# A two-layer hybrid trunk: the narrow projection columns beside the retention's first head, a re-ordered opening, and four output buffers

## The chip, the cores and the metric

One Trainium2 chip, one core. The metric is the device time of one execution in microseconds; lower is better. TensorE multiplies matrices into PSUM, VectorE (DVE) and ScalarE (ACT) work on tiles in SBUF and PSUM, GpSimd (POOL) does little here, and SyncE (SP) issues every DMA from one queue.

## What is computed

Two layers over 512 latent tokens and 256 context tokens, 1024 features wide. A layer modulates its input, multiplies it by one wide `w_in`, feeds the columns to three mixers (a state-space mixer, SSD; latent attention, MLA; retention), multiplies the joined results by `w_out`, and normalises.

```python
sh_l, sc_l, g_l = jnp.split(mod_l[:, None, :], 3, axis=-1)   # mod = silu(c) @ w_ada + b_ada
h_l = x * (1 + sc_l) + sh_l
parts_l = jnp.split(h_l @ w_in[i], in_splits(), axis=-1)
...
IN_WIDTHS = (SSD_WIDTH, SSD_CONV_DIM, SSD_HEADS,
             MLA_Q_LORA, MLA_KV_LORA, MLA_ROPE_DIM, MLA_WIDTH,
             RET_QK_WIDTH, RET_QK_WIDTH, RET_WIDTH, RET_WIDTH)
...
dtc = jax.nn.softplus((dt_c + dt_bias)).reshape(...)          # SSD_HEADS = 16 columns
v = v.reshape(b, n, RET_HEADS, 1, RET_V_DIM)                  # RET_WIDTH = 512 columns, 4 heads of 128
out_l = jnp.concatenate([ssd_l, mla_l, ret_l], -1) @ w_out[i]
x_new = layer_norm(ALPHA * x + g_l * out_l, ln_g, ln_b)
```

Two of the projected pieces are narrow: 16 columns `dt` of the SSD and 32 columns `kr`, the rotary part of the MLA keys. Each token's context part is computed in layer 0 and, as keys and states only, in layer 1.

## The kernel before

**Data.** Tokens are columns: features `h` lie as eight tiles `hh[k]`, `hl[k]` of 128 features x 768 tokens (256 context columns first, then 512 latent ones). Each is a split of a float32 tile into a rounded part (`hh`, type fp32r) and a remainder (`hl`), and so are weights (`wh`, `wl`). `mm3` (L145) makes a product of three matmuls: hi x hi, hi x lo, lo x hi.

**Weights.** `wslot` (L153) loads 128 x 1024 floats of weights into one of two staging buffers `wr`, rounds them on ScalarE (`wh`) and subtracts on VectorE (`wl`), with three buffers each; from the seventh call on with high priority. `pslot` (L163) does the same in buffers of a given pool. The tile framework orders each engine's instructions ahead of time; each engine then runs its own list in order, waiting on semaphores. SP's list holds all loads and stores, so a load that waits for a buffer holds those behind it.

**A projection.** `proj` (L171) keeps 128 x 128 of weights stationary and moves 512 latent and then 256 context columns of `hh`, `hl` past them, for k = 0 to 7: 24 matmuls over 512 and 24 over 256 columns. It takes accumulators from `acc`, three PSUM banks.

**The opening** (`start`, layer 0). For k = 0 to 7 `ada(0, (j, j + 8))` multiplies two 512 KB tiles of `w_ada` (`ar`) with the conditioning vector and turns the result into columns `mod`; `make_h0(k)` loads `x`, modulates it with the columns k and 8 + k, and splits it into `hh[k]`, `hl[k]`; then three projections advance by one k, with accumulators `p0` (latent) and `c0` (context). Their tiles are `M_T` (the 48 narrow columns `dt` and `kr`), `B_T` and `B_T + 2` (the SSD's B and C of the first group). `ada` for k = 0 and k = 1 come before `make_h0(0)`, and all three weights go through `wslot`.

**The dt stage** (`dt_stage`, L439). In layer 0 it takes the opening's results (`first`); in layer 1 it projects `rq0`, `rq1` and C over the latent columns (`proj_lat`, interleaved by k while the normalisation before is still writing `hh`), then the narrow tile and B with `proj_many`. ScalarE copies the narrow rows into `ms` (48 x 768), six transposes (L470) turn them to tokens by rows, and a chain on VectorE makes `dt`, cumulative sums and decays. `pad` copies a projection with margins into one of three `xpad` buffers, from which `conv` works.

**The retention's values** (`ret_v`, step `rv0`). Here `hh` is stationary: for each of 2 halves of the 512 columns and each of 6 chunks of 128 tokens, 24 matmuls move 256 columns of weights over 128 stationary token columns. VectorE sums each head (`vm`), ScalarE subtracts the mean into `stv`, and SP stores it to `rv`.

**Order.** `STEPS` (L48) lists the steps of a layer: `dt0 xbc0 ... rv0 ssd1 ...`. `xbc` convolves B, C and four tiles `X_T`..., `ssd` runs the state-space chunks, the others project and store.

**The end** (`ln_turned`, layer 1). Four matmul groups `pot` give 128 x 512 outputs; VectorE scales each into `ho`, from two buffers shared under the tag `hr`, and SP stores it.

## Time and profile before

| | us |
|---|---|
| timed runs | 1483.25, 1487.1, 1488.01 (median 1487.1) |
| the profiled execution | 1483.76 |
| its span, first to last instruction | 1481.8 |
| TensorE busy | 1426.5 (96%) |
| VectorE busy | 1076.6 (73%) |
| ScalarE busy | 692.6 (47%) |
| mean granted TensorE clock | 0.987 of full |

The profile is one execution. A busy share is an average over stages. A matmul's recorded length overlaps its neighbours', so how long a row of matmuls takes is read from their starts. A weight load (PEld) runs beside the matmul before it. The granted clock is 1.00 at 2.4 GHz and 0.50 at 1.2 GHz. The number in brackets behind a row is the idle time of its engine just before, with what ended it.

### The profile page before, as it was taken

Reading aid. Unit: us, or ns where it says so; the run is one execution under the profiler, and the core shown is the slowest. Engines: PE = TensorE matmul, PEld = TensorE weight load, DVE = VectorE, ACT = ScalarE, POOL = GpSimd, SP = SyncE. Lnnn points to the kernel's source line nnn. Section 1 sums busy time; section 2 is a strip of 40 time slices with the busy share of each in tenths; the row PEclk is TensorE's granted clock in tenths of the full one; section 3 lists DMA queues with packets and bytes.
Section 4 is the critical chain, followed back from the end, with each engine's and each line's share of the span. In section 5 each row is a group of like instructions: output and inputs, shape, how many; then the busy total and the mean of one; then the engine's idle time right before and its main releaser. Section 6 shows DMA issues by size and latency. Waiting matters only on the chain. (4 is left out here: it accounts for less than half of the span.)

```text
span 1481.8 us, 23394 instructions
## 1 busy us (share of the span) xinstructions
PE 1426.5 (96%) x8696; PEld 1158.2 (78%) x8696; DVE 1076.6 (73%) x2077; ACT 692.6 (47%) x1377; POOL 25.7 (2%) x35
## 2 busy tenths in 40 slices
PE   6999999999999999999999899999999999989988
PEld 4787789778888888777788778788778887767667
DVE  3599894995486667678645858997776767678846
ACT  2346743662232443477622345565463344347742
POOL 0000000000000001000001000000000000100010
PEclk9999999999999999999999999999999999999999
DMA  8336553457725746624241223353357465562241
GB/s 337 138 99 180 183 168 110 158 184 256 258 72 175 247 154 198 222 82 131 80 170 58 91 88 111 120 148 114 98 168 251 136 199 190 171 205 89 69 141 57
DMA packets 109725, 226.18 MB, mean 153 GB/s; under 512 B 13534, under 2 KB 41310, under 8 KB 109356
## 3 DMA queue, kind: packets, MB, share of 16 engines
q1 hardware_dynamic: 109612, 224.70, 46.5%
q8 instruction: 68, 1.11, 0.3%
q14 instruction: 45, 0.37, 0.1%
HBM read 174.46 MB, written 50.20 MB: 152 GB/s over the span
## 5 line engine op out<-in xcount | busy, mean ns | idle before, releaser
L101 PE MATMUL pj<-hh,wh 128*128 128x512 f32 (+1 forms) x984 | 354.5, 361 | 2.8 <-ACT hh L115 2.4
L101 PE MATMUL pj<-hh,wl 128*128 128x512 f32 (+1 forms) x984 | 353.2, 359 | 0.0
L101 PE MATMUL pj<-hl,wh 128*128 128x512 f32 (+1 forms) x984 | 350.7, 356 | 0.0
L122 ACT CAST wh<-wr 128x1024 fp32r<-128x1024 f32 (+1 forms) x116 | 120.3, 1039 | 208.8 <-PE pj L101 92.2
L101 PEld LDWEIGHTS pj<-hh,wh 128*128 128x128 f32 x984 | 185.1, 188 | 36.0 <-issue 8.9
L101 PEld LDWEIGHTS pj<-hh,wl 128*128 128x128 f32 x984 | 185.0, 188 | 31.2 <-issue 7.0
L101 PEld LDWEIGHTS pj<-hl,wh 128*128 128x128 f32 x984 | 185.2, 188 | 30.5 <-issue 6.4
L104 DVE TENSOR_TENSOR wl<-wr,wh 128x1024 fp32r<-128x1024 f32 (+1 forms) x116 | 141.0, 1216 | 79.6 <-ACT wh L122 78.5
L104 DVE TENSOR_TENSOR pel<-pe,peh 128x512 fp32r<-128x512 f32 (+1 forms) x112 | 71.6, 648 | 37.0 <-ACT peh L115 36.5
L107 DVE SCALAR_TENSOR_TENSOR cv<-xpad,cw,cv 128x772 f32<-128x772 f32 (+1 forms) x96 | 92.2, 993 | 0.2
L115 ACT ACTIVATE pe<-psc 128x512 f32<-128x512 f32 (+1 forms) x112 | 63.7, 569 | 56.4 <-PE psc L101 47.6
L1043 DVE TENSOR_REDUCE nm<-pmx 128x1 fp32r<-128x768 f32 (+1 forms) x80 | 67.6, 845 | 15.7 <-PE pmx L101 14.5
L101 PE MATMUL po<-sh,wh 128*128 128x512 f32 (+1 forms) x192 | 70.0, 367 | 4.2 <-DVE oy L107 4.2
L101 PE MATMUL po<-sl,wh 128*128 128x512 f32 (+1 forms) x192 | 70.1, 366 | 1.9 <-DVE sl L107 1.9
L115 ACT ACTIVATE ce<-cf 64x512 f32<-64x512 f32 (+1 forms) x80 | 46.9, 587 | 50.3 <-DMA cf<-cum 49.5
L101 PE MATMUL po<-sh,wl 128*128 128x512 f32 (+1 forms) x192 | 69.6, 364 | 0.0
L115 ACT ACTIVATE tm<-sf,dt 128x128 f32<-128x128 f32 x160 | 52.5, 390 | 30.4 <-DVE sf L104 30.3
L115 ACT ACTIVATE peh<-psc 128x512 fp32r<-128x512 f32 (+1 forms) x112 | 63.6, 568 | 0.2
L101 PE MATMUL po<-mr,wh 128*128 128x256 f32 (+1 forms) x216 | 55.5, 343 | 3.1 <-DVE la L107 3.1
L115 ACT ACTIVATE arg<-arg,ncb 128x128 f32<-128x128 f32 x160 | 54.9, 393 | 4.1 <-DVE arg L107 3.6
L101 PE MATMUL pv<-wl,hh 128*128 128x256 f32 x192 | 54.0, 281 | 0.7 <-DVE wl L104 0.7
L101 PE MATMUL pv<-wh,hh 128*128 128x256 f32 x192 | 53.7, 280 | 0.0
(337 smaller groups left out, 2952.1 us busy)
## 6 DMA issues: line engine op xcount, KB each, us to landing
wr<-in_win SPq DMA_DIRECT2D x82, 512.0 KB, 3.8
ar<-in_wada SPq DMA_DIRECT2D x48, 512.0 KB, 7.0
cf<-cum SPq DMA_DIRECT2D x80, 256.0 KB, 4.6
wr<-in_wout SPq DMA_DIRECT2D x32, 512.0 KB, 4.3
y<-ys SPq DMA_DIRECT2D x20, 256.0 KB, 2.5
xs<-th SPq DMA_DIRECT2D x16, 256.0 KB, 2.1
x<-in_xT SPq DMA_DIRECT2D x8, 384.0 KB, 8.6
rv<-stv SPq DMA_DIRECT2D x24, 128.0 KB, 3.0
```

What stands on the lines that cost most here:

```text
L101: return self.nc.tensor.matmul(out, lhsT=lhsT, rhs=rhs, start=start, stop=stop, **k)
L104: return self.nc.vector.tensor_tensor(out, a, b, op=op)
L107: return self.nc.vector.scalar_tensor_tensor(out, in0=a, scalar=s, in1=b, op0=op0, op1=op1)
L115: return self.nc.scalar.activation(out, in_, f, **k)
L122: self.nc.scalar.copy(hi, raw)
L1043: nc.vector.tensor_reduce(nm[:, i:i + 1], p1[:, 0:n], axis=AX.X, op=ALU.max, negate=True)
```

## The change

1. The narrow tile is no more. Its 48 columns stand behind the 128 of the retention's first head: `ret_v(0)` moves 176 columns, 704 of a slot's 1024 floats per half of k. `ret_v(1)` moves heads 1 and 2 (256 columns), `ret_v(2)` head 3 (128 columns, one slot for all k, stored where `M_T` was). `ret_v(0)` runs in `dt_stage`, the other two in step `rv0`. The chunks go latent first. A copy per chunk puts the 48 columns into `mt`, tokens by rows, so `dt` needs no transpose; `kr` is transposed back, 32 columns a chunk.
2. The opening projects `B_T`, `B_T + 2` and `X_T`. `ada` for k = 0 is followed by `make_h0(0)` and the weight loads, then by `ada` for k = 1. The third weight tile goes through `pslot`. Layer 0's `dt_stage` pads all three.
3. In layer 1 `ret_v(0)` follows `proj_lat`, and B is projected by itself behind it.
4. `ho` has a tag of its own with four buffers.

```diff
--- before.py
+++ after.py
@@ -315,19 +315,22 @@
 
     def start(self, P):
 
-        tiles = ((M_T, 48), (B_T, 128), (B_T + 2, 128))
+        tiles = ((B_T, 128), (B_T + 2, 128), (X_T, 128))
         lat = [self.acc.tile([128, 512], F32, tag="acc", name="p0") for _ in tiles]
         cx = [self.ps("cx", "c0", 3) for _ in tiles]
         ws = []
         for k in range(KD):
-            for j in (0, 1) if k == 0 else (k + 1,):
-                if j < KD:
-                    self.ada(0, (j, j + 8), P)
-            self.make_h0(P, k)
-            if not ws:
+            if k == 0:
+                self.ada(0, (0, 8), P)
+                self.make_h0(P, 0)
                 for t, m in tiles:
-                    ws.append([x[:, :8 * m].rearrange("p (k c) -> p k c", k=8)
-                               for x in self.wslot(self.A["win"][0, t][:, :8 * m], 8 * m)])
+                    src = self.A["win"][0, t]
+                    w = self.pslot(P, src, 1024) if t == X_T else self.wslot(src)
+                    ws.append([x.rearrange("p (k c) -> p k c", k=8) for x in w])
+            if k + 1 < KD:
+                self.ada(0, (k + 1, k + 9), P)
+            if k:
+                self.make_h0(P, k)
             for ps, a, b in ((lat, NCTX, T), (cx, 0, NCTX)):
                 for p, (hi, lo), (t, m) in zip(ps, ws, tiles):
                     self.mm3(p[:m, 0:b - a], [(hi[:, k, :], lo[:, k, :], self.hh[k][:, a:b], self.hl[k][:, a:b])],
@@ -422,7 +425,8 @@
         elif n == "ssd":
             self.ssd(i)
         elif n == "rv":
-            self.ret_v()
+            self.ret_v(1)
+            self.ret_v(2)
         elif n == "mod":
             self.pending = [(0, (j, j + 1)) for j in range(16, 24, 2)] + [(1, (j, j + 1)) for j in range(0, 24, 2)]
         else:
@@ -447,33 +451,30 @@
             nc.vector.memset(xp[:, 774:776], 0.0)
         self.cnt = 0
         if l == 0:
-            first = self.first
+            self.padded = {t: self.pad(p) for t, p in zip((B_T, B_T + 2, X_T), self.first)}
         else:
             rq0, rq1, pc2 = self.proj_lat(l, (RQ_T, RQ_T + 1, B_T + 2))
             self.store(D["rq"][0], rq0)
             self.store(D["rq"][1], rq1)
             self.padded = {B_T + 2: self.pad(pc2)}
-            first = self.proj_many(l, [(M_T, 48), (B_T, 128)]) + [None]
-        self.pre = {B_T: first[1], B_T + 2: first[2]}
-        ms = S.tile([48, T], F32, tag="u", name="ms", bufs=2)
-        for p, a, b in first[0]:
-            self.copy(ms[:, a:b], p)
-        if l == 0:
-            self.padded = {}
-        for t in (B_T, B_T + 2):
-            if t not in self.padded:
-                self.padded[t] = self.pad(self.pre[t])
-        self.load(D["kr"], ms[0:32, :])
-        pt = self.ps("tr", "pt", 2)
-        ptv = pt[:, 0:288].rearrange("p (c h) -> p c h", c=NCH)
-        for c in range(NCH):
-            nc.tensor.transpose(ptv[:, c, :], ms[:, c * 128:(c + 1) * 128], self.ident[:48, :48])
+
+        mt = S.tile([128, XC], F32, tag="u", name="mt", bufs=2)[:, 0:NCH * 48].rearrange("p (c m) -> p c m", c=NCH)
+        self.ret_v(0, mt)
+        if l:
+            self.padded[B_T] = self.pad(self.proj(l, B_T))
+        kt = S.tile([32, T], F32, tag="u", name="kt", bufs=2)
+        for a, b in ((2, 6), (0, 2)):
+            pt = self.ps("tr", "pt", 2)
+            for c in range(a, b):
+                nc.tensor.transpose(pt[0:32, (c - a) * 128:(c - a + 1) * 128], mt[:, c, 0:32], self.ident)
+            self.copy(kt[:, a * 128:b * 128], pt[0:32, 0:(b - a) * 128])
+        self.load(D["kr"], kt)
         n = 2 * NCH * 16
         mk = lambda nm: S.tile([128, 2, NCH, 16], F32, name=nm)
         fl = lambda t: t.rearrange("p d c h -> p (d c h)")
         x, e, s, q = mk("dtx"), mk("dte"), mk("dts"), mk("dtq")
         for d in range(2):
-            self.tt(x[:, d], ptv[:, :, 32:48],
+            self.tt(x[:, d], mt[:, :, 32:48],
                     pc[:, P_DT + 16 * d:P_DT + 16 * d + 16].unsqueeze(1).to_broadcast([128, NCH, 16]), ALU.add)
         self.ts(fl(e), fl(x), -1.0, ALU.mult)
         self.tt(fl(e), fl(e), fl(x), ALU.min)
@@ -666,27 +667,35 @@
         self.load(D["y"][g][:, :, c * 128:(c + 1) * 128].rearrange("t p i -> p t i"), ys)
 
 
-    def ret_v(self):
+    def ret_v(self, n, mt=None):
+
         l = self.l
-        for n in range(2):
-            sl = [self.wslot(self.A["win"][l, RV_T + n * 2 + j]) for j in range(2)]
-            sl = [(a.rearrange("p (k c) -> p k c", k=4), b.rearrange("p (k c) -> p k c", k=4)) for a, b in sl]
-            for c in range(NCH):
-                p = self.acc.tile([128, 512], F32, tag="acc", name="pv")
-                cs = slice(c * 128, (c + 1) * 128)
-                self.mm3(p[:, 0:256], [(self.hh[k][:, cs], self.hl[k][:, cs], sl[k // 4][0][:, k % 4, :],
-                                        sl[k // 4][1][:, k % 4, :]) for k in range(KD)])
-                with self.tc.high_priority():
-                    st = self.sp.tile([128, 256], F32, tag="stv", name="stv", bufs=2)
-
-                    vm = self.sp.tile([128, 2], F32, tag="vm", name="vm", bufs=2)
-                    self.nc.vector.tensor_reduce(vm, p[:, 0:256].rearrange("p (h e) -> p h e", e=128), axis=AX.X,
-                                                 op=ALU.add, negate=True)
-                    self.ts(vm, vm, 1.0 / 128, ALU.mult)
-                    for h in range(2):
-                        self.act(st[:, h * 128:h * 128 + 128], p[:, h * 128:h * 128 + 128], AF.Identity,
-                                 bias=vm[:, h:h + 1])
-                    self.load(self.D["rv"][:, c, n * 256:(n + 1) * 256], st)
+        h0, nh = ((0, 1), (1, 2), (3, 1))[n]
+        w = 128 * nh + (48 if n == 0 else 0)
+        if n < 2:
+            sl = [self.wslot(self.A["win"][l, RV_T + 2 * n + j][:, 0:4 * w], 4 * w) for j in range(2)]
+            sl = [[x[:, 0:4 * w].rearrange("p (k c) -> p k c", k=4) for x in y] for y in sl]
+        else:
+            x = [y.rearrange("p (k c) -> p k c", k=8) for y in self.wslot(self.A["win"][l, M_T])]
+            sl = [[y[:, 0:4] for y in x], [y[:, 4:8] for y in x]]
+        for c in (2, 3, 4, 5, 0, 1):
+            p = self.acc.tile([128, 512], F32, tag="acc", name="pv")
+            cs = slice(c * 128, (c + 1) * 128)
+            self.mm3(p[:, 0:w], [(self.hh[k][:, cs], self.hl[k][:, cs], sl[k // 4][0][:, k % 4, :],
+                                  sl[k // 4][1][:, k % 4, :]) for k in range(KD)])
+            with self.tc.high_priority():
+                if n == 0:
+                    self.copy(mt[:, c], p[:, 128:176])
+                st = self.sp.tile([128, 256], F32, tag="stv", name="stv", bufs=2)
+
+                vm = self.sp.tile([128, 2], F32, tag="vm", name="vm", bufs=2)
+                self.nc.vector.tensor_reduce(vm[:, 0:nh], p[:, 0:128 * nh].rearrange("p (h e) -> p h e", e=128),
+                                             axis=AX.X, op=ALU.add, negate=True)
+                self.ts(vm[:, 0:nh], vm[:, 0:nh], 1.0 / 128, ALU.mult)
+                for h in range(nh):
+                    self.act(st[:, h * 128:h * 128 + 128], p[:, h * 128:h * 128 + 128], AF.Identity,
+                             bias=vm[:, h:h + 1])
+                self.load(self.D["rv"][:, c, h0 * 128:(h0 + nh) * 128], st[:, 0:128 * nh])
 
 
     def blocks(self):
@@ -1287,7 +1296,7 @@
             fs = slice(512 * f, 512 * f + 512)
             for c in range(k):
                 self.mm(po[c, f], nd[:, c * 128:(c + 1) * 128], lgr[:, fs], False, True, skip_group_check=True)
-                o = P.tile([128, 512], F32, tag="hr", name="ho", bufs=2)
+                o = P.tile([128, 512], F32, tag="ho", name="ho", bufs=4)
                 self.stt(o, po[c, f], y[:, c:c + 1], lbr[:, fs], ALU.mult, ALU.add)
                 self.load(self.out[1][c * 128:(c + 1) * 128, fs], o)
 
@@ -1369,11 +1378,12 @@
     for l in range(L):
         for i, s in enumerate(starts):
             W[l, i] = kmajor(win[l, :, s:s + 128], 128)
-        for n in range(2):
-            for j in range(2):
-                W[l, RV_T + n * 2 + j] = kmajor(win[l, j * 512:(j + 1) * 512, 4272 + n * 256:4272 + (n + 1) * 256], 256)
-        m = np.concatenate([win[l, :, 3216:3248], win[l, :, 2560:2576]], 1)
-        W[l, M_T, :, :384] = kmajor(m, 48)
+        v = win[l, :, 4272:4784]
+        m = np.concatenate([v[:, 0:128], win[l, :, 3216:3248], win[l, :, 2560:2576]], 1)
+        for j in range(2):
+            W[l, RV_T + j, :, :704] = kmajor(m[j * 512:(j + 1) * 512], 176)
+            W[l, RV_T + 2 + j] = kmajor(v[j * 512:(j + 1) * 512, 128:384], 256)
+        W[l, M_T] = kmajor(v[:, 384:512], 128)
     o["win"] = W
     uq = f["mla_w_uq"].reshape(L, 384, 8, 96)
     cols = np.concatenate([uq[..., :64].reshape(L, 384, 512), uq[..., 64:].reshape(L, 384, 256)], -1)
```

## Rows read from the trace of the kernel before

**Rows 1.** The page: busy time by engine; shares of the chain that ended last.
```profile
PE 1426.5 (96%) x8696; PEld 1158.2 (78%) x8696; DVE 1076.6 (73%) x2077; ACT 692.6 (47%) x1377; POOL 25.7 (2%) x35
...
PE pj L101 14%; PE po L101 4%; PE ppv L101 2%; PE psc L101 2%; PE pstate L101 1%; PE pv L101 1%; PE pq L101 1%; DVE cv L107 1%; DVE wl L104 1%; PE pin L101 1%; PE prs L101 1%; PE py L101 1%; DMA cf<-cum 1%; ACT wh L122 1%; PE pry L101 1%
```

**Rows 2.** Timeline, TensorE (start, length, line, op, out<-in): narrow tile, then `ret_v`.
```profile
859.76 0.39 PE L101 MATMUL pj<-hh,wh 128*48 128x512 f32 x1
...
859.99 0.40 PE L101 MATMUL pj<-hl,wh 128*48 128x512 f32 x1
...
1033.06 0.28 PE L101 MATMUL pv<-wh,hh 128*128 128x256 f32 x1
...
1034.00 0.28 PE L101 MATMUL pv<-wh,hl 128*128 128x256 f32 x1
```

**Rows 3.** Weight loads by shape: busy us, mean ns of one, idle before.
```profile
L101 PEld LDWEIGHTS pv<-wh,hh 128*128 128x128 f32 x192 | 36.1, 188 | 0.0
...
L101 PEld LDWEIGHTS pcol<-ones,nx 128*128 128x128 f32 x44 | 5.2, 191 | 1.3 <-DVE nx L104 1.0 <-issue 0.3
...
L101 PEld LDWEIGHTS pnm<-identr,nm 128*1 128x1 f32 x80 | 5.1, 82 | 6.6 <-ACT bqh L118 3.2 <-DVE nm L1043 0.7 <-issue 0.7
...
L470 PEld LDWEIGHTS pt<-K,ms 48*128 48x128 f32 x12 | 0.9, 138 | 1.9 <-ACT ms L118 1.8
```

**Rows 4.** Timeline, TensorE: four matmuls moving 128 columns over one weight column.
```profile
608.64 0.40 PE L101 MATMUL pnm<-identr,nm 128*1 128x128 f32 x4 [1.47 <-ACT bqh L118]
```

**Rows 5.** Timeline, TensorE: one-column moves, transposes, and `pv` after a stall.
```profile
57.85 0.57 PE L470 MATMUL pt<-K,ms 48*128 48x48 f32 x6 [1.60 <-ACT ms L118]
...
1032.71 0.39 PE L101 MATMUL pv<-wl,hh 128*128 128x256 f32 x1 [0.68 <-DVE wl L104]
...
1032.94 0.28 PE L101 MATMUL pv<-wh,hl 128*128 128x256 f32 x1
...
1470.64 0.58 PE L101 MATMUL pcol<-ones,lxs 128*128 128x1 f32 x4
```

**Rows 6.** Groups by shape, VectorE, whole span.
```profile
L683 DVE TENSOR_REDUCE vm<-pv 128x2 f32<-128x256 f32 x24 | 10.1, 422 | 22.6 <-PE pv L101 22.4
```

**Rows 7.** Timeline, all engines, the opening.
```profile
10.65 0.34 DVE L112 TENSOR_SCALAR mod<-pm,pc 128x2 f32<-128x2 f32 x2 [6.68 <-PE pm L101]
...
13.81 0.86 DVE L112 TENSOR_SCALAR x<-x,mod 128x512 f32<-128x512 f32 x2
...
15.16 0.33 SPq L98 DMA_DIRECT2D wr<-in_win  x1
...
25.33 0.40 DVE L112 TENSOR_SCALAR x<-x,mod 128x256 f32<-128x256 f32 x1
...
26.65 0.89 PE L101 MATMUL p<-hh,wh 128*48 128x512 f32 x3 [1.07 <-ACT hh L122]
```

**Rows 8.** Windows: stretch, length, busy us of the engines, granted clock, DMA share, GB/s.
```profile
2.00:14.00 12.00, 5.21 (x68) 3.71 (x68) 1.31 (x9) 1.26 (x5) 0.00 (x0) 1.00 0.94 343
...
14.00:16.00 2.00, 0.41 (x1) 0.23 (x2) 1.57 (x4) 1.30 (x2) 0.00 (x0) 1.00 0.08 31
...
18.00:44.00 26.00, 24.45 (x230) 17.36 (x232) 11.38 (x24) 6.28 (x10) 0.00 (x0) 1.00 1.02 406
...
59.00:63.00 4.00, 4.00 (x12) 3.18 (x12) 3.80 (x7) 1.06 (x2) 0.00 (x0) 0.57 0.47 149
```

**Rows 9.** Timeline, the end of the opening.
```profile
58.80 0.50 PE L101 MATMUL pj<-hh,wh 128*128 128x512 f32 x1 [0.38 <-ACT wh L122]
...
58.80 1.21 DVE L104 TENSOR_TENSOR wl<-wr,wh 128x1024 fp32r<-128x1024 f32 x1
```

**Rows 10.** Timeline, the tail.
```profile
1473.05 4.37 PE L101 MATMUL pot<-lgr,nd 1*128 1x512 f32 x8
...
1477.15 1.56 DVE L107 SCALAR_TENSOR_TENSOR ho<-pot,rp_y,lbr 128x512 f32<-128x512 f32 x2 [1.33 <-DMA out<-ho]
```
## Prediction

> **What bounds the kernel now.** I read the page first: TensorE is busy for 1426.5 us, 96% of the span, and in the chain that ended last matmuls have the largest share, the projections `pj` ahead of all [rows 1]. So TensorE is the bound nearly everywhere, and an edit is worth what it does to the time from one matmul start to the next, to TensorE's stalls, and to the stretches at the lower of its two clocks (1.2 and 2.4 GHz). Next I read the timeline for start-to-start times [rows 2] and the weight loads by shape [rows 3], then the timelines of the opening, its end, the start of layer 1 and the tail. Recorded matmuls overlap, so only starts are used below.
>
> **Narrower retention chunks.** Before, a layer's `ret_v` is 12 chunks of 24 matmuls, each moving 256 columns over 128 stationary columns of `hh` or `hl`. They start 0.117 us apart (eight steps from 1033.06 to 1034.00 [rows 2]), so 288 x 0.117 = 33.7 us. After, it is 18 chunks: six move 176 columns, six 256, six 128. The stationary side stays 128 columns, so the question is whether a matmul that moves fewer than 256 columns over 128 stationary ones starts sooner than 0.117 us after the last. The trace has none in this data type. It bounds it so. From below: with a one-column weight, 128 moving columns start (0.40 - 0.22)/3 = 0.060 us apart [rows 4] (0.22 is the recorded length of a single one, taken off here and below); scaled from 256 columns in 0.117, 176 would take 0.080. From above: weight loads. A 128-column load lasts 188 ns in this type and 191 in plain float32, a one-column load 82 [rows 3]: a fixed part near 82 and 106 for the columns. Whether the recorded length is real shows in three places [rows 5]. Plain float32 matmuls that move one column over 128 weight columns start (0.58 - 0.25)/3 = 0.11 us apart although they move next to nothing. Transposes, whose 128-column load is recorded as 138 (56 above the fixed part [rows 3]), start (0.57 - 0.23)/5 = 0.07 apart. And after a stall in `pv`, where no load could run ahead, the second matmul starts 0.23 us after the first in place of 0.12: its own load of 0.11 lies open. So I take 0.112 us for both narrow widths, by the rows with the same weight width, and keep 0.060 to 0.117 for the bounds. Then `ret_v` is 144 x (0.112 + 0.117 + 0.112) = 49.1 us, **+15.4 a layer**.
>
> The Trainium skill (TensorE: Matmul & The Clock Gate, Back-to-back issue gap) gives about 81 ns for each load-and-matmul pair that moves 128 columns, which speaks against this; by it, as an estimate, both narrow sorts would cost 81, `ret_v` 40.2 us, and the whole sum would end near 1475. The open load of 0.11 us in `pv` [rows 5] is longer than that whole figure, so here the trace differs.
>
> **The narrow tile goes.** Its projection, 48 output columns, still moves 512 and then 256 columns: 24 x (0.232 + 0.117) = 8.4 us (48-column matmuls over 512 start 0.23 apart [rows 2]). In layer 1 it disappears; in layer 0 the opening computes an `X_T` tile of the same moving size in its place, and that tile disappears from `xbc0`. **-8.4 a layer**. The six transposes that follow now move 128 columns and not 48: bounded by 0.07 (no change) and twice that, at about 0.12, **+0.3 a layer** [rows 5]. Together 2 x (15.4 - 8.4 + 0.3) = **+14.6 us**.
>
> What rides along: reduces go from 12 to 18 a layer, of 0.42 us at two heads [rows 6]; six copies `mt` replace the two `ms`; `stv` activations keep their number; stores of `rv` go from 12 to 18 on SP with the same bytes. Nothing: a chunk has 2.7 us of matmuls as cover, and three accumulators. Without that cover about twice a reduce, 0.8 us a chunk, would lie open. The `dt` chain starts some 16 us of `ret_v` later in layer 0; the three padded tiles give VectorE convolutions to do meanwhile, and TensorE has later projections queued. Nothing; bounds -4 to +4 for single stalls of the SSD stages that may vanish or appear, about 1 us each.
>
> **The opening.** Before, SP issues a third weight load at 15.16 us only, when a staging buffer comes free [rows 7]. Everything behind it in SP's queue waits, `x` of the second feature tile among it; DMA, at 343 GB/s from 2 to 14 us, fell to 31 in the next two [rows 8]. The second tile's matmuls begin at 26.65 [rows 7], and from there TensorE is full to the end of the opening near 56.3, 29.7 us. After, the third weight tile has a buffer of its own, so nothing blocks. Ahead of the second `x` lie about 0.5 MB of constants, six modulation tiles and three weight tiles (128 x 1024 floats, 512 KB each) and two `x` (128 x 768, 384 KB), 6.0 MB. Before, 4.1 MB had come by 14 us (343 GB/s for 12 us); the rest at 400, as from 18 to 44 [rows 8], takes it to 18.8. From the start of `x`'s modulation to the matmuls are 1.8 us (0.46 for its first part, 1.32 from 25.33 to 26.65 [rows 7]), so they can start at 20.6; the first tile, free from its neighbour's modulation (11.0 and not 13.8 [rows 7]), is done by then. I take 21: **-5.6**. Ends: -7.3 (19.3, no idle between the first two tiles) and 0 (VectorE's in-order queue again, as when the second `x`'s last part waited to 25.33 behind the third tile's `mod` [rows 7]).
>
> **End of the opening.** TensorE stops at about 56.3, runs six transposes and gets going again at 58.80, held by the cast `wh` [rows 9], which had to wait for one of three weight slots; then, from 59 to 63, its granted clock averages 0.57 [rows 8], 4 x 0.43 = 1.7 us lost. After, the third slot is free during the opening, so the first half of `ret_v(0)`'s weights can be split ahead; the second half still waits for a slot, ScalarE and VectorE, with 1.4 us of matmuls as cover. Of 2.3 + 1.7 I take **-2**; ends 0 and -4.
>
> **Start of layer 1.** Before, a 384-column split stood between `proj_lat` and the next matmuls, and TensorE didn't stop there (starts 0.23 apart [rows 2]). Now it is 704 columns twice, behind slots that come free together: by the 1.21 us of a 1024-column subtraction on VectorE [rows 9], 0.8 us each, so **+1**, between 0 and +2.
>
> **Tail.** With four `ho` buffers the third scaling need not wait 1.33 us for a store, but the last `pot` ends at 1477.4 and the last of four scalings ended at 1478.7 [rows 10]: **-0.5**, ends 0 and -1.3.
>
> **Sum.** 14.6 - 5.6 - 2 + 1 - 0.5 = **+7.5 us**. Against the profiled execution, 1483.8 us, its span 1481.8, that is 1491.3. That execution is among the lower ones: the three timed runs are 1483.25, 1487.1 and 1488.01. The middle of the four is 1485.4, and from there the sum gives **1493**.
>
> **Rivals.** (1) *Time follows the moving width*, faster. Place: the 288 narrow matmuls of a layer. At 0.060 and 0.080 `ret_v` is 37.0 us, 5.1 below the 42.1 of before with the narrow tile; the sum is -16.6, **1469**. For it: the one-column rows [rows 4]. Against: the open load [rows 5]. It decides below 0.099 us a narrow matmul, where the sum is zero. Chance 0.08. The Trainium skill's 81 ns (TensorE: Matmul & The Clock Gate, Back-to-back issue gap) is a milder form of this case and has its chance here. (2) *The opening pays in full*: -7.3 and -4, sum +3.8, **1489**, within the bound of a measurement. For it: the hole in DMA is there to be closed, 2 us long, and the low clock behind the opening too [rows 8]. Against: in-order queues. 0.20. (3) *The opening doesn't do what it says*: other loads or `mod` order VectorE and SP as before; sum +15.1, **1500.5**. 0.06. (4) *Short moves lose their single pass* and take plain float32's rate: a 128-column move at 0.112, a 176-column one then at 0.147; +10, **1503**. Against: 0.060 for 128 columns [rows 4]. 0.04.
>
> **Numbers.** The forecast has 0.62, of which 0.53 lies more than 0.3% (4.5 us) above before; 0.3% is about what a measurement of this kernel can tell from no change. Faster: 0.08 of (1) and 0.01 of (2), with 0.01 of the forecast. Same: 0.16 of (2), 0.08 of the forecast, 0.01 of (3). Slower: 0.53, 0.03 of (2), 0.05 of (3), 0.04 of (4). So 0.10, 0.25, 0.65. The range 1484 to 1502 takes in the forecast with the bounds of opening and stalls, (2) and (3), and leaves out (1), (4) and little else.
>
> **What would show it.** In the profile after: `pv` starts about 0.112 us apart at 176 and 128 columns (0.060 to 0.080 means rival 1, 0.147 rival 4); `ret_v(0)` near 16 us in both layers; the second feature tile's first matmul near 21 us, the opening's last near 51, and no SP issue blocked between 6 and 15; no 1.2 GHz stretch behind the opening, or a short one; layer 1's first retention chunk starting with up to 1 us of idle before it. I am wrong if narrow starts come closer than 0.099, or if the opening gives back more than 11 us.

## The result

The changed kernel takes 1505.33 us (median of 4 runs, 1504.18 to 1506.89) against 1485.82 for the kernel before on the same chip; the ratio is 1.0131, 95% interval 1.0109 to 1.0154. So it is slower by 19.5 us where the forecast said 7.5, and the time lies above the range. The profiled spans differ by 20.6 us (1502.4 against 1481.8).

The page of the profile after, busy us of each engine (the line answers to the first of [rows 1]): TensorE has 192 matmuls more and is still the bound, 96% of a longer span.

```profile
PE 1443.5 (96%) x8888; PEld 1178.5 (78%) x8888; DVE 1081.1 (72%) x2101; ACT 694.8 (46%) x1389; POOL 25.7 (2%) x35
```

To find where the 20.6 us lie, I cut both spans at the same TensorE events, read from the timelines.

| from, to | before | after | difference | forecast |
|---|---|---|---|---|
| span's start, opening's last matmul | 55.98 | 56.04 | +0.1 | -5.6 |
| to the next matmul of a stage | 58.80 | 57.24 | -1.6 | -2 |
| to layer 0's last value matmul | 260.1 | 271.1 | +12.6 | +7.3 |
| to layer 0's last matmul | 833.7 | 847.0 | +2.3 | 0 |
| to layer 1's last value matmul | 1048.1 | 1070.4 | +9.0 | +8.3 |
| to the span's end | 1481.8 | 1502.4 | -1.7 | -0.5 |

The second and third columns are the times at which each stage ends. Two lines miss by much: the opening gives nothing, and layer 0 up to its last value matmul loses 5.3 us more than the steps account for.

**The value passes.** Timeline of TensorE in the changed kernel (start, length, line, op, out<-in), layer 1's passes of 176 and of 128 columns; answers to [rows 2].

```profile
874.25 0.27 PE L101 MATMUL pv<-wh,hl 128*128 128x176 f32 x1
...
875.48 0.27 PE L101 MATMUL pv<-wl,hh 128*128 128x176 f32 x1
...
1054.64 0.27 PE L101 MATMUL pv<-wh,hl 128*128 128x128 f32 x1
...
1055.20 0.28 PE L101 MATMUL pv<-wl,hh 128*128 128x128 f32 x1
```

Eleven steps of 176 columns in 1.23 us and five of 128 in 0.56: both 0.112 apart, as forecast, and hardly less than the 0.117 of 256 columns.

**The opening.** Timeline of VectorE and TensorE; answers to [rows 7].

```profile
12.89 0.79 PE L101 MATMUL p<-hh,wh 128*128 128x512 f32 x1 [2.21 <-ACT hh L122]
...
21.10 0.34 DVE L112 TENSOR_SCALAR mod<-pm,pc 128x2 f32<-128x2 f32 x2 [4.86 <-PE pm L101]
22.94 0.35 DVE L112 TENSOR_SCALAR mod<-pm,pc 128x2 f32<-128x2 f32 x2 [1.49 <-PE pm L101]
23.20 0.86 DVE L112 TENSOR_SCALAR x<-x,mod 128x512 f32<-128x512 f32 x2
...
24.98 1.09 PE L101 MATMUL p<-hh,wh 128*128 128x512 f32 x2 [1.53 <-ACT hh L122]
```

The first feature tile comes 2.7 us sooner (12.89 against 15.59). The second needs its own modulation values, which are there at 21.10; but VectorE's next instruction is the third tile's values, which come at 22.94, and only behind them stands the second tile's `x`. So its matmuls start at 24.98, where 21 was forecast and 26.65 is the row of before. Then the clock falls. Windows of the changed kernel: stretch, length, busy us of the engines, granted clock, DMA share, GB/s.

```profile
24.00:28.00 4.00, 3.02 (x8) 2.45 (x9) 2.20 (x5) 1.66 (x2) 0.00 (x0) 0.64 1.03 403
```

A granted clock of 0.64 of 2.4 GHz means that part of the stretch ran at 1.2 GHz. The 1.7 us that the second tile had won are gone at the opening's last matmul.

The first tile is slow too. Timeline of TensorE: two of its steps of 512 columns.

```profile
16.99 0.63 PE L101 MATMUL p<-hh,wl 128*128 128x512 f32 x1
17.42 0.63 PE L101 MATMUL p<-hl,pwh 128*128 128x512 f32 x1
```

They start 0.43 us apart, as such steps do in the low stretch behind the second tile; at the full clock they take 0.23. The clock column has 1.00 there, but its records in this trace begin only at 18.3. The small matmuls for the second tile's values stand among the first tile's, at 17.98 and 19.59, so they come late with it.

**Layer 0 behind the opening.** Timeline: the first value matmul (answers to [rows 9]), the first convolution `cv`, the copy into a padded tile, and TensorE waiting for that copy.

```profile
57.24 0.35 PE L101 MATMUL pv<-wh,hh 128*128 128x176 f32 x1 [0.92 <-ACT xpad L118]
...
89.26 0.68 DVE L112 TENSOR_SCALAR cv<-xpad,cw 128x772 f32<-128x772 f32 x1 [1.82 <-DMA cum<-ct]
...
94.67 0.86 ACT L118 COPY xpad<-pj 128x512 f32<-128x512 f32 x2 [6.03 <-DVE cv L107]
95.31 0.39 PE L101 MATMUL pj<-hh,wh 128*128 128x256 f32 x1 [1.77 <-ACT xpad L118]
```

Between 57 and 73 us TensorE does the first value pass, and the convolutions that should fill VectorE meanwhile do not run. The first starts at 89.26 (before: 75.79, row below), behind the whole `dt` chain, for which the last narrow columns come at 73. All three padded tiles are full until then, so the next x tile's copy waits 6.03 us for a convolution and TensorE waits for the copy. Timeline of VectorE in the kernel before; then windows of the changed kernel.

```profile
75.79 0.69 DVE L112 TENSOR_SCALAR cv<-xpad,cw 128x772 f32<-128x772 f32 x1 [2.02 <-ACT ct L118]
...
59.00:63.00 4.00, 4.00 (x38) 4.00 (x37) 1.76 (x4) 2.28 (x8) 0.00 (x0) 1.00 0.31 105
96.00:101.00 5.00, 5.00 (x30) 4.91 (x29) 4.22 (x5) 3.08 (x8) 0.00 (x0) 0.66 0.00 0
```

Two more things stand in this line of the table. The low clock that stood right behind the opening (59 to 63, 0.57 before) is gone there, but a stretch of the same cost, some 1.6 us, comes behind the wait for the copy. And of the modulation steps (groups of small `pr` matmuls) that are spread over layer 0, eight now stand ahead of its last value matmul, where six did before: by the starts some 0.7 us each, so about 1.4 of the 5.3 us are moved there from behind that matmul.

**Layer 1 and the tail.** Timeline: the first value matmuls of layer 1, and the last scalings (answer to [rows 10]).

```profile
873.13 0.83 PE L101 MATMUL pv<-wh,hh 128*128 128x176 f32 x2
874.06 0.35 PE L101 MATMUL pv<-wl,hh 128*128 128x176 f32 x1
...
1495.09 1.54 DVE L107 SCALAR_TENSOR_TENSOR ho<-pot,rp_y,lbr 128x512 f32<-128x512 f32 x2 [1.08 <-PE pot L101]
...
1498.71 0.75 DVE L107 SCALAR_TENSOR_TENSOR ho<-pot,rp_y,lbr 128x512 f32<-128x512 f32 x1 [0.96 <-PE pot L101]
```

From 873.13 to 874.25 three steps take 1.12 us in place of 0.34: 0.8 us of waits, where 1 was forecast. In the tail no scaling waits for a store any more; they wait for TensorE instead.

### The profile page after: what moved, and what is told of

It reads as the page before. It is cut to its first block, busy times and chain, and to the rows that moved or that the text cites. A ratio compares the mean times of both kernels' runs of the same rounds, so it can differ in the third digit from the quotient of the medians.

```text
span 1502.4 us, 23851 instructions
## 1 busy us (share of the span) xinstructions
PE 1443.5 (96%) x8888; PEld 1178.5 (78%) x8888; DVE 1081.1 (72%) x2101; ACT 694.8 (46%) x1389; POOL 25.7 (2%) x35
## 5 line engine op out<-in xcount | busy, mean ns | idle before, releaser
L101 PE MATMUL pj<-hh,wh 128*128 128x512 f32 (+1 forms) x952 | 342.4, 360 | 4.2 <-ACT hh L115 2.4
L101 PE MATMUL pj<-hl,wh 128*128 128x512 f32 (+1 forms) x952 | 342.5, 360 | 0.0
L101 PE MATMUL pj<-hh,wl 128*128 128x512 f32 (+1 forms) x952 | 341.1, 358 | 0.0
L101 PEld LDWEIGHTS pj<-hh,wh 128*128 128x128 f32 x952 | 180.5, 190 | 35.9 <-issue 8.1
L101 PEld LDWEIGHTS pj<-hl,wh 128*128 128x128 f32 x952 | 180.5, 190 | 29.8 <-issue 7.2
L101 PEld LDWEIGHTS pj<-hh,wl 128*128 128x128 f32 x952 | 180.6, 190 | 28.8 <-issue 6.4
L101 PE MATMUL pv<-wh,hh 128*128 128x176 f32 (+2 forms) x288 | 79.9, 277 | 1.0 <-ACT xpad L118 0.9
L101 PE MATMUL pv<-wh,hl 128*128 128x176 f32 (+2 forms) x288 | 79.7, 277 | 0.0
L101 PE MATMUL pv<-wl,hh 128*128 128x176 f32 (+2 forms) x288 | 79.5, 276 | 0.1
L115 ACT ACTIVATE arg<-arg,ncb 128x128 f32<-128x128 f32 x160 | 55.2, 393 | 10.5 <-DVE arg L107 10.0
```

Of the source, the lines that this page charges most:

```text
L101: return self.nc.tensor.matmul(out, lhsT=lhsT, rhs=rhs, start=start, stop=stop, **k)
L115: return self.nc.scalar.activation(out, in_, f, **k)
```

## The experiments

My theory after the two traces: the matmul steps came as forecast; the opening's reordering brought nothing since VectorE's order holds the second tile; and layer 0 pays for a late `dt` chain. The rivals: that the steps cost something else than I think, or that the clock or later stages took the time. Each kernel is an edit of the changed one; times are medians, and ratios are to the kernel before on the same chip. An interval is some 5 us wide on each side, so single microseconds are read from the traces, which show one execution each.

**1. The opening in its old order.**

```
-            if k == 0:
-                self.ada(0, (0, 8), P)
-                self.make_h0(P, 0)
+            for j in (0, 1) if k == 0 else (k + 1,):
+                if j < KD:
+                    self.ada(0, (j, j + 8), P)
+            self.make_h0(P, k)
+            if not ws:
...
```

> Edit on the changed kernel: the opening is emitted in the order of before (both first modulations, then the first feature tile, then its weights), with the changed kernel's three weight tiles. Theory from the traces (the reordered opening ends where the old one did, 56.04 against 55.98, because the second tile still comes late and TensorE fills the time after it without a gap): last matmul at 55.5 to 57, 1505 +- 1.5. Rival (the prediction's step: the new order is worth 5.6 us, and something else in the changed opening, such as its third full-width tile, took that back): 1509 to 1512.

Measured: 1505.81 us, ratio 1.0125 (1.0094 to 1.0155), the changed kernel's own time. Timeline of TensorE: the second tile's first matmul and the opening's last.

```profile
26.77 0.73 PE L101 MATMUL p<-hh,wh 128*128 128x512 f32 x2 [1.53 <-ACT hh L122]
...
56.31 0.28 PE L101 MATMUL c<-hh,pwl 128*128 128x256 f32 x1
```

The old order ends at 56.31 and the new one at 56.04. It starts the second tile 1.8 us later, takes 29.5 us from there instead of 31.1, and has no low clock there. So the new order is worth 0.3 us in this pair, not 5.6. Its second tile wins 1.8 us, and the low clock takes 1.5 of them back; the third full-width tile takes nothing.

**2. The second tile ahead of the third's modulation.** Three edits try to let VectorE go on to the second tile. First, for all tiles:

```
-            if k + 1 < KD:
-                self.ada(0, (k + 1, k + 9), P)
             if k:
                 self.make_h0(P, k)
+            if k + 1 < KD:
+                self.ada(0, (k + 1, k + 9), P)
```

> Edit on the changed kernel: in the opening each feature tile from the second on is loaded and modulated before the modulation of the next tile is computed, so that its modulation stands ahead of the next tile's small additions on VectorE. Theory (VectorE's order holds the second tile): in the changed kernel the second tile's own modulation values are there at 21.10 and VectorE is idle until 22.94, where it waits for the third tile's values; only then it modulates the second tile (23.20), and TensorE starts on it at 24.98. Here that start should come at 23.2 to 23.3, the opening's last matmul 1.7 us earlier than 56.04, or 3.4 earlier if the low-clock stretch after the start goes too: 1502 to 1503.6 in all, against 1505.3. Rival (the opening's end is set elsewhere, by the loads or by TensorE's total work): last matmul at 56.0 as before and after, 1505 +- 1.

Measured: 1506.87 us, ratio 1.0133 (1.0097 to 1.0169). The second tile comes at 23.47 and the clock stays up, yet the last matmul is at 56.53. Timelines: VectorE's modulation of three later tiles, and TensorE within one of them.

```profile
41.27 0.35 DVE L112 TENSOR_SCALAR mod<-pm,pc 128x2 f32<-128x2 f32 x2 [1.86 <-PE pm L101]
...
51.21 0.35 DVE L112 TENSOR_SCALAR mod<-pm,pc 128x2 f32<-128x2 f32 x2 [1.86 <-PE pm L101]
...
42.70 0.28 PE L101 MATMUL c<-hh,pwl 128*128 128x256 f32 x1
42.91 0.64 PE L101 MATMUL pr<-ar,sil 128*32 128x128 f32 x16
43.48 0.74 PE L101 MATMUL p<-hh,wh 128*128 128x512 f32 x2
```

Two tiles take 9.94 us, 4.97 each; in the changed kernel they take 4.64 (41.12, 45.76, 50.40). The modulation's small float32 matmuls are now in two groups a tile, not one. Around each group a gap of 0.2 stands for 0.12 on the way in, and on the way out another 0.1 each on the last small matmul and on the first large one: about 0.3 us a change of kind, there and back, six times over, 2 us. From its second tile to the end the opening takes 33.1 us, where the changed kernel's takes 29.5 when its clock stays up (experiment 3). Most of the rest is the third tile's modulation, which the changed kernel does while it waits for the second tile: behind that tile's start there are now 176 small `pr` matmuls in place of 150, some 1.7 us with their row products.

Second, only the two small additions that end a modulation were put later:

```
-                self.ada(0, (k + 1, k + 9), P)
+                mod = self.ada(0, (k + 1, k + 9), P, True)
             if k:
                 self.make_h0(P, k)
+            if k + 1 < KD:
+                mod()
```

> Edit on the changed kernel: only the two small additions that finish the next tile's modulation are put behind the current tile's modulation on VectorE; loads and TensorE's order stay those of the changed kernel, and its 16 small modulation matmuls a tile stay in one group. Theory (in the run with the whole step put first, the second tile did come 1.5 us sooner, but each tile then took 4.97 us instead of 4.64, because its 16 small matmuls were split in two groups and each change between the two kinds of matmul costs TensorE 0.3 us): here the second tile comes at 23.3 and the tiles stay 4.64 apart, so the opening's last matmul is at 54.3, or at 52.7 if the stretch of low clock at 25 goes as well: 1502 to 1503.6. Rival (the tile's period lengthens whenever the tile comes earlier, since the loads or the chain behind the modulation set it): last matmul at 56, 1505 +- 1.5.

Measured: 1501.3 us, ratio 1.0106 (1.0074 to 1.0139), an interval that overlaps the changed kernel's; what lies under the lower median is open, its opening does not explain it. VectorE's timeline shows that the edit did not do what it says: one of the two additions still stands ahead of `x`, at 23.00.

```profile
23.00 0.22 DVE L112 TENSOR_SCALAR mod<-pm,pc 128x2 f32<-128x2 f32 x1 [1.49 <-PE pm L101]
23.13 0.86 DVE L112 TENSOR_SCALAR x<-x,mod 128x512 f32<-128x512 f32 x2
```

The second tile starts at 24.91 and the opening ends at 56.17. This run tells nothing on the rival. Third, the second tile alone goes first:

```
+            if k == 1:
+                self.make_h0(P, k)
             if k + 1 < KD:
                 self.ada(0, (k + 1, k + 9), P)
-            if k:
+            if k > 1:
                 self.make_h0(P, k)
```

> Edit on the changed kernel: for the second feature tile alone the modulation is emitted ahead of the third tile's modulation values; from the third tile on the order is the changed kernel's. In the first of the two earlier attempts on this queue all tiles were split in two groups of small matmuls, in the second one of the two small additions still stood ahead of the tile. Theory (VectorE's order holds the second tile by 1.7 us, and the order of the later tiles is better left): second tile at 23.2 to 23.6, one split (0.3 us), then 4.64 a tile; last matmul of the opening at 53.0 to 53.5 without a low-clock stretch behind the gap, 54.5 to 55 with one, against 56.04: 1502 to 1504. Rival (the end of the opening is set by something else): 55.5 to 56.5, 1505 +- 1.5.

Measured: 1511.24 us, ratio 1.0150 (1.0117 to 1.0182). Timelines: the second and third tile's first matmuls, and VectorE between them.

```profile
22.04 0.73 PE L101 MATMUL p<-hh,wh 128*128 128x512 f32 x2 [1.63 <-ACT hh L122]
...
26.36 0.35 DVE L112 TENSOR_SCALAR mod<-pm,pc 128x2 f32<-128x2 f32 x2 [3.38 <-PE pm L101]
29.82 0.34 DVE L112 TENSOR_SCALAR mod<-pm,pc 128x2 f32<-128x2 f32 x2 [3.12 <-PE pm L101]
30.09 0.86 DVE L112 TENSOR_SCALAR x<-x,mod 128x512 f32<-128x512 f32 x2
...
31.86 0.73 PE L101 MATMUL p<-hh,wh 128*128 128x512 f32 x2 [1.52 <-ACT hh L122]
```

The second tile comes at 22.04, sooner than expected. Now the third has to wait in the same way: its values are there at 26.36, the fourth tile's stand ahead of its `x` and come at 29.82, TensorE gets it at 31.86, 9.8 us behind the second, and the opening ends at 58.34. This run also has two stretches of low clock in its opening (0.66 from 22 to 27 us and again from 32 to 37), some 1.7 us each.

So VectorE's order is what holds a tile: shown twice, for two tiles. It is not what sets the opening's end. With the second tile at 23.47, 22.04 and 23.04 (second run of experiment 7) the opening ended at 56.53, 58.34 and 54.79; the changed kernel's own order, where its clock stayed up, had the second tile at 23.95 and 24.30 and ended at 53.48 and 53.87 (experiments 3 and 6). By the rows, what TensorE does while it waits for the second tile must be done behind it when the tile comes sooner; no run shows that alone.

**3. The late `dt` chain.** A projection that needs no padded tile goes ahead of the x tiles:

```
-STEPS = ("dt0 xbc0 ssd0 rk0 rq0 ...
+STEPS = ("dt0 rk0 xbc0 ssd0 rq0 ...
```

> Edit on the changed kernel: in layer 0 one projection that needs no convolution (the retention's first key tile, 8.4 us of TensorE) is computed ahead of the first x tiles instead of behind the first SSD group. Theory (TensorE's waits of 1.36 and 2.17 us at 82 and 93 come from the three padded tiles, all held until the convolution of B, which stands behind the late dt chain): the key tile fills that time, the wait at 93 goes and the one at 82 may stay: 1501.5 to 1503.5. Rival (the first SSD group needs the x tiles, and putting them 8.4 us later delays it as much): the waits come back between 115 and 190, 1504 to 1509.

Measured: 1500.18 us, ratio 1.0090 (1.0061 to 1.0118). The wait for a padded tile is gone. From the first value matmul to the last of layer 0 it takes 208.5 us (54.68 to 263.2); the changed kernel takes 213.9 and the kernel before, with 7.3 us less of steps, 201.3. So this one move gives back 5.4 us, as much as layer 0 loses there beyond its steps. About 3.8 of them are waits and small gaps, and 1.6 are the low stretch behind the wait, which is gone too (1.00 from 93 to 101); of the eight kernels here that have this wait of 1.8 us, the changed one among them, four have the stretch. Its opening, which the edit does not touch, ended at 53.48; two steps of the first tile and the window show why.

```profile
16.53 0.39 PE L101 MATMUL p<-hh,wl 128*128 128x512 f32 x1
16.76 0.40 PE L101 MATMUL p<-hl,pwh 128*128 128x512 f32 x1
...
24.00:28.00 4.00, 4.00 (x40) 3.41 (x40) 2.62 (x4) 0.83 (x1) 0.00 (x0) 1.00 1.02 403
```

The first tile's steps are down to 0.23 already, so the second tile comes 1.0 us sooner, and the clock is full where the changed kernel had 0.64, another 1.5. Of the 6.2 us between the two profiled spans these 2.5 are luck of the clock, the edit gives 5.4, and 1.7 are lost again behind layer 0's values.

The other way is to let the convolutions run in the first pass, as the prediction had it:

```
         self.ret_v(0, mt)
...
+        if l == 0:
+            self.convbc(0)
         kt = S.tile([32, T], F32, tag="u", name="kt", bufs=2)
...
-            ct = S.tile([16, T], F32, tag="cv", name="ct", bufs=2)
+            ct = S.tile([128, 2, 4, 128], F32, tag="ce", name="ct", bufs=2)...[0:16, 0:T]
```

> Edit on the changed kernel: in layer 0 the convolutions of B and C are put ahead of the dt chain in the program, and ct gets a buffer that no convolution uses. Theory (the first convolutions stand behind the dt chain, which now waits for the narrow columns): the first convolution moves from 89.3 into the first value pass (57 to 75), the three padded tiles come free sooner, TensorE's waits at 82.2 (1.36) and 93.1 (2.17) go, and the kernel gains 3 to 5 us: 1500 to 1502.5. Rival (what the SSD stage needs is the end of the dt chain itself, which cannot move): these waits go, but as much idle time comes back later in layer 0, 1505 +- 1.5.

Measured: 1512.06 us, ratio 1.0157 (1.0118 to 1.0196); neither side expected a loss. Timelines of VectorE and TensorE, and the window behind.

```profile
70.62 2.07 DVE L107 SCALAR_TENSOR_TENSOR cv<-xpad,cw,cv 128x772 f32<-128x772 f32 x2
72.62 0.28 DVE L701 TENSOR_REDUCE vm<-pv 128x1 f32<-128x128 f32 x1
...
74.34 0.51 PE L101 MATMUL pv<-wh,hh 128*128 128x176 f32 x1 [4.76 <-ACT stv L115]
...
72.00:86.00 14.00, 11.65 (x55) 11.34 (x56) 6.17 (x17) 3.97 (x11) 0.00 (x0) 0.51 0.14 43
```

The convolutions do start early, at 58. Now the reduce of a value chunk stands behind them on VectorE, the chunk's accumulator stays taken, and TensorE waits 4.76 us; the clock falls in that wait, and TensorE is busy for 11.65 us at about half of full speed, some 6 us lost. The cover that the prediction counted on would not have been free even if it had been there.

**4. Layer 1 as before.**

```
-        self.ret_v(0, mt)
+        if l == 0:
+            self.ret_v(0, mt)
+        else:
+            first = self.proj_many(l, [(M_T, 48), (B_T, 128)])
...
```

> Edit on the changed kernel: layer 1 goes back to a narrow tile of its own and two value passes of 256 columns; layer 0 and the opening stay changed. Theory (the passes of 176 and 128 moving columns cost as much a step as one of 256): layer 1 loses one pass of 144 steps of 0.112 us (16.1) and gets 72 steps of 0.117 back (8.4), and its six transposes of 128 columns become six of 48: 7.5 to 8 us less of steps, with up to 1.8 us of waits at the layer's start on top: 1495.5 to 1498. Rival (most of the time of the change comes from waits and clock, not from the number of steps): 1501 to 1505.

Measured: 1503.41 us (1499.22 to 1506.75), ratio 1.0114 (1.0077 to 1.0151): in the range of the rival, above that of the theory. The trace, of the fastest execution (1499.22), tells the parts apart. Timeline of TensorE: layer 0's last matmul and layer 1's last value matmul.

```profile
845.93 0.28 PE L101 MATMUL po<-mh,wl 128*128 128x256 f32 x1
...
1061.30 0.28 PE L101 MATMUL pv<-wh,hl 128*128 128x256 f32 x1
```

From layer 0's last matmul to layer 1's last value matmul it takes 215.4 us (845.9 to 1061.3), in the changed kernel 223.4 (847.0 to 1070.4). So the layer gains 8.0 us, as the steps and the start's waits have it. Behind that point it is 436.1 against 432.0, with 31 us of stretches at half clock against 25, 3 us lost of those 4. In this execution the step count is right, and the clock hides a good part of it in the total; that it does so in the other three too is not shown.

**5. What sets a narrow step.** Half of the stationary columns:

```
+            m = 64 if n == 2 else 128
+            cs = slice(c * 128, c * 128 + m)
-            self.mm3(p[:, 0:w], ...
+            self.mm3(p[:m, 0:w], ...
```

> Edit on the changed kernel: the third value pass (head 3, 128 moving columns, 144 steps a layer) loads 64 stationary columns instead of 128; half the tokens of that head are left out, their rows of the result are not written. Theory (a step of 128 moving columns takes 0.112 us because its stationary load of 128 columns takes that long): steps start 0.060 to 0.075 us apart, 5.3 to 7.5 us a layer less, 1490 to 1495. Rival (a floor of about 0.11 us for any short step of this kind, whatever is loaded): 0.112 apart, 1505 +- 1.5.

Measured: 1501.43 us, ratio 1.0094 (1.0059 to 1.0129). Timeline: steps of the third pass, a wait in it, and what ScalarE waited for; last, the weight load's group (busy us, mean ns).

```profile
1053.65 0.22 PE L101 MATMUL pv<-wh,hh 128*64 128x128 f32 x1
...
1053.96 0.23 PE L101 MATMUL pv<-wh,hl 128*64 128x128 f32 x1
...
265.00 0.36 ACT L115 ACTIVATE stv<-pv,vm 64x128 f32<-64x128 f32 x1 [3.81 <-DMA rv<-stv]
...
265.42 0.28 PE L101 MATMUL pv<-wh,hh 128*64 128x128 f32 x1 [1.28 <-ACT stv L115]
...
L101 PEld LDWEIGHTS pv<-wh,hh 128*64 128x64 f32 x96 | 13.9, 145 | 6.2 <-ACT stv L115 6.2
```

Five steps in 0.31 us, 0.062 apart; over the whole run the median is 0.060. The moving columns are the same 128, and the load's own mean falls from 188 ns [rows 3] to 145, so the 0.112 is the stationary load of 128 columns: the theory's mechanism is shown. The time is another matter: 1490 to 1495 was expected. At 1.4 us a chunk instead of 2.7 the pass runs into its eviction. The two `stv` buffers wait for their stores, ScalarE waits for them, and TensorE for ScalarE. A row says so (1.28); what was a free follower at 2.7 us a chunk is the bound at 1.4. The edit has a share in that: it stores the 64 rows of a chunk twice, to both halves of its place (the text ahead of the run says that half is not written), so there are two stores a chunk.

The other end, wider steps:

```
-        h0, nh = ((0, 1), (1, 2), (3, 1))[n]
+        h0, nh = 2 * n, 2
         w = 128 * nh + (48 if n == 0 else 0)
+        for i, m in enumerate((4, 4) if n else (3, 3, 2)):
+            y = self.wslot(self.A["win"][l, RV_T + 3 * n + i][:, 0:m * w], m * w)
...
```

> Edit on the changed kernel: the narrow columns stand beside two heads instead of one, so the passes have 304 and 256 columns (two passes, not three); the weights of the first lie in three slots of 3, 3 and 2 blocks. Theory (below 256 columns a step costs what the stationary load costs, above it what its columns cost): steps of 304 columns start 0.139 us apart (on the line from 0.117 at 256 to 0.232 at 512), a layer's passes take 144 x (0.139 + 0.117) = 36.9 us instead of 49.1, two layers -24.4, less 0 to 2 us a layer for the third slot, which leaves no buffer for loads ahead: 1481 to 1485, a little under the kernel before. Rival (the step's time jumps where the columns leave a size that one pass takes, to that of 512): 0.232 a step, 50.3 us a layer, 1507 to 1510.

Measured: 1481.54 us, ratio 0.9959 (0.9943 to 0.9975): as expected, and under the kernel before. Timeline of TensorE: steps of 304 columns, and the wait that is left.

```profile
59.77 0.30 PE L101 MATMUL pv<-wl,hh 128*128 128x304 f32 x1
...
61.45 0.30 PE L101 MATMUL pv<-wh,hl 128*128 128x304 f32 x1
...
100.70 0.58 PE L101 MATMUL pj<-hh,wh 128*128 128x256 f32 x1 [4.17 <-ACT xpad L118]
```

Twelve steps in 1.68 us, 0.14 apart. Above 256 columns a step costs what its columns cost, so 48 columns more beside two heads cost 0.023 a step, where beside one head they cost a whole extra pass. The wait for the padded tile is there too, 4.17 us, longer than in the changed kernel since the first pass is longer.

**6. The tail.**

```
-                o = P.tile([128, 512], F32, tag="ho", name="ho", bufs=4)
+                o = P.tile([128, 512], F32, tag="hr", name="ho", bufs=2)
```

> Edit on the changed kernel: the output tile at the end has two buffers, shared with the tag of before, instead of four of its own. Theory (the prediction's term): the third and fourth scaling wait for a store again, 0.5 to 1.3 us at the end: 1505.5 to 1506.8. Rival (nothing waits, the two stores end the run at the same time): 1505.3 +- 1.

Measured: 1507.08 us (1499.9 to 1508.75), ratio 1.0116 (1.0085 to 1.0146), no difference that the times could tell. In its trace the wait of 1.3 us for a store is back, and from the first scaling to the span's end it takes 7.4 us (1496.5 to 1503.9) against 7.3 in the changed kernel: the waits for TensorE cover it, and the four buffers are worth 0.1.

**7. The gains together.** The wide passes with the key tile first:

> Edit on the changed kernel: the two edits that moved it most, together: the narrow columns beside two heads (passes of 304 and 256 columns), and in layer 0 the first key tile ahead of the first x tiles. Theory: the wide version alone took 1481.5 and shows TensorE's waits of 0.80 and 4.57 us at 86.8 and 96.1, which the key tile fills: 1476.5 to 1479. Rival (they come back where the first SSD group needs the x tiles): 1480 to 1482.

Measured: 1477.79 us (1474.22 to 1481.19), ratio 0.9931 (0.9908 to 0.9955). From the first value matmul to layer 0's last it is 197.3 us (57.6 to 254.9), less than the 201.3 of before: the wait of 4.17 us is gone and no single one over 1 us came in its place. And with `ct` in a buffer of its own and the loads of the opening put in another order:

```
                 for t, m in tiles:
+                    if t == X_T:
+                        self.ada(0, (1, 9), P)
                     src = self.A["win"][0, t]
...
```

> Edit on the changed kernel: as the wide version with the key tile first, and in addition ct in a buffer that the convolutions do not use, and an opening in which the second tile's modulation loads stand ahead of the third weight tile and its modulation ahead of the third tile's. Theory: the first convolution no longer waits 1.8 us for the store of ct, and the second feature tile comes at 20.8 to 22 instead of 24.3, so that the opening's last matmul is at 51 to 53.5 instead of 55.2: 1472 to 1476. Rival (the opening's start is not what sets its end, and the store's wait is hidden): as without these two, 1476.5 to 1479.

Measured: 1479.17 us, ratio 0.9934 (0.9909 to 0.9958), the same as without these two. The second tile's matmuls start at 23.04 and the opening ends at 54.79, where 51 to 53.5 was expected. Timeline of TensorE: the third weight tile, now last in the queue, holds the first feature tile instead.

```profile
20.13 0.50 PE L101 MATMUL p<-hh,pwh 128*128 128x512 f32 x1 [0.56 <-ACT pwh L122]
...
21.39 0.50 PE L101 MATMUL p<-hh,pwl 128*128 128x512 f32 x1 [0.29 <-DVE pwl L104]
```

Both are faster than the kernel before and, by more, than the changed one.

## Why the prediction was wrong, step by step

**Right: the steps of `ret_v` and the narrow tile, +14.6.** The widths of 176 and 128 columns start 0.112 us apart, as taken from the rows with the same weight width; half a stationary side brings 0.060 and 304 columns 0.14. Layer 1 with its old passes is 8.0 us shorter, where the steps and the start's waits had 7.3 + 1. Layer 1's 8.0 is read from one trace; its time of 1503.41 does not confirm it. The first and the fourth rival fall with this.

The Trainium skill (TensorE: Matmul & The Clock Gate, Back-to-back issue gap) has about 81 ns for such a pair that moves 128 columns. The trace does not agree for steps of this kind: they took 112.

**Right: the end of the opening and the start of layer 1.** -1.6 where -2 was taken, and 0.8 where 1 was. The -2 was taken out of 2.3 us of wait and 1.7 us of low clock. The wait gave the 1.6; the low clock went as well, but it lies in the next line of the table, where the stretch behind the copy's wait stands against it.

**Wrong: the opening, -5.6.** It was 0.1, near the upper bound of 0, for which the prediction had named VectorE's order; it gave that case, the third rival, a chance of 0.06. The failed step is the one from the second `x`'s load to its matmuls, for which only 1.8 us of `x`'s own modulation and cast were counted. Its modulation values also pass through TensorE, behind the first tile's matmuls, and its modulation stands behind the next tile's values: 24.98 in place of 21. A second step failed with it, "from there TensorE is full to the end", 29.7 us whenever the second tile comes. Here it took 31.1, 1.5 of them by the low clock, which ate what was won; and where the edits brought the tile sooner still, more work stood behind it (experiments 2 and 7). The old order of emission gives the same end within 0.3 us (experiment 1).

**Wrong: "the `dt` chain starts later ... Nothing".** Layer 0 loses 5.3 us beyond its steps up to its last value matmul. The step that failed is the cover: "the three padded tiles give VectorE convolutions to do meanwhile". They stand behind the chain in VectorE's program, and they are what frees the padded tiles for which TensorE then waits. Moving other TensorE work there gives 5.4 us back (experiment 3); running the convolutions in that place costs more than it gives. Of the 5.3 some 1.4 are modulation steps that only stand earlier now, which the prediction did not have either.

**Mis-sized: the tail**, 0.1 where 0.5 was taken.

With the measured terms the sum is 14.6 + 0.1 - 1.6 + 5.3 + 0.8 - 0.1 = 19.1 us, against 20.6 in the spans and 19.5 in the medians. The rest is not settled: 0.9 in layer 1 up to its last value matmul, beyond the steps and the start, and the two lines of the table where the change has no step, +2.3 in the second part of layer 0 (with two modulation steps fewer) and -1.7 behind layer 1's values. The range ended at 1502 because it took in each miss alone: the third rival gives 1500.5 and the bound on stalls is 4 us, and in this run the opening gave nothing and layer 0 lost its 5.3 us, both at once.

## What to carry to other kernels

Before columns are moved from a tile of their own to the side of another, look up which side sets the step: while the stationary load sets it, a narrow pass costs as much as one of twice the width, and the columns are cheapest beside the widest pass that there is. When a chain of small steps starts later, do not ask whether there is other work for its engine but what stands ahead of that work in the engine's own order, and which buffers it frees. And let a range hold the sum of two misses, not the larger of them.

## What the runs showed that I had not expected

- The same opening ran with and without a stretch at 1.2 GHz. In the changed kernel and five of the kernels above (experiments 3, second, 4, both of 5, and the first of 7) the clock fell at 24 to 27 us and the opening ended between 55.2 and 56.7; in two others (experiment 3, first, and 6) it did not fall, and the opening ended at 53.48 and 53.87. In the changed kernel and in the first of experiment 3 TensorE was idle for the same 1.53 us just before; between 18 and 24 us it was busy for 4.58 us in the one that fell and 3.59 in the one that did not. One thing does divide the eight: in the two where the clock stayed up, the first tile's steps of 512 columns were 0.23 apart from 16.3 and 16.7 us on; in the six where it fell, steps that began between 16.57 and 17.29 still took 0.43. That this is the cause is not shown, and with another order of the opening (experiment 2, third) the clock was up by 16.1 and fell at 22.6 all the same.
- A change between the opening's large matmuls and its small float32 ones costs TensorE about 0.3 us there and back (experiment 2), so that splitting each tile's group in two took 2 us over six tiles.
